# Order of the cross-attention weight products around an output projection, in a fused encoder layer

## The chip, the cores and the metric

The kernel runs on one core of a Trainium2 chip. The metric is the device time of one execution in microseconds; before the change it is 1414.73 us, the median of three runs (1414.48 to 1418.52).

The engines are called as in the profile: PE (TensorE, matrix products), DVE (VectorE), ACT (ScalarE), POOL (GpSimd) and SP (SyncE, which issues most loads). PE writes its results to PSUM, which has eight banks of 128 x 512 float32; DVE and ACT empty them.

## The reference

One encoder layer on 1024 tokens of width 1024, in float32, with 256 memory tokens:

```
x = x + rms_norm(concat(rms_norm(s5(u)), rms_norm(fox(q, k, v))) @ w_out)
h = rms_norm(x)
q = h @ wq                                   # 4 heads of 256
k, v = split(rms_norm(mem) @ wkv)            # 256 memory tokens
p = softmax(q k^T / 16) per head
x = x + rms_norm((p v, heads side by side) @ wo)
x = x + rms_norm(swiglu(rms_norm(x)))
```

s5 is a state-space mixer on half of the channels, fox a forgetting attention with 8 heads on the other half.

## The kernel before, in words

Products are made in about full precision: each operand is split into a high and a low part (`split`, L112: ACT copies the source into the rounded high part, DVE subtracts it from the source for the low part), and each product is three matmuls (`mm3`, L121: high x high, high x low, low x high; lines L122, L123, L124).

The cross-attention is rearranged so that no query or value matrix is made for the tokens. For each head, wq is multiplied by the keys beforehand (`build_a`, L993): one 1024 x 256 matrix per head that turns a token tile directly into scores. `build_a(0)` makes heads 0 and 1, `build_a(1)` heads 2 and 3; the result is kept in the tiles Ah and Al. In the same way each head's values are multiplied by its rows of wo (the "value weights", VW, L1207 to L1224), so that a token tile's softmax weights times VW gives the projected output directly.

The order around the change is this:

1. The forgetting attention runs with other work between its units (L1014 to L1016): the state-space branch's projections, the memory's keys and values (written to DRAM as kv_d), the SSM half of the output projection (written to DRAM as t1_d), and at its end `build_a(0)`.
2. The output projection's attention half (L1033 to L1058, "the projection loop"): eight tiles of 128 tokens in the order 3, 4, 5, 6, 7, 0, 1, 2, each in two half tiles of 512 columns. A half tile is twelve matmuls into one PSUM bank "x" (L1045). DVE adds the SSM half, fetched from t1_d into the tile t (L1039, called t_d in the profile), with the factor r_f per row (L1046); r_f exists only when the forgetting attention is complete. ACT sums squares (L1048), POOL multiplies by a gain row (L1050), and after both halves DVE makes the row's norm factor (L1052, L1053) and adds the residual (L1054). The tile goes to DRAM for tiles 3 to 7 (L1058) and is kept in SBUF for 0 to 2. After each half tile one step of `build_a(1)` is taken (L1051): a step is twelve matmuls of 256 columns. There are eight steps, so the written order has them in the first half of the loop.
3. The value weights of the four heads, one after the other (L1208 to L1224): 24 matmuls of 512 columns per head, in four banks (g for even heads, x for odd ones); the head's second half of the contraction (d = 1) follows after all four banks have had the first. Tile 0's norm is prepared and its transposes are made with the last head (L1210, L1222).
4. Scores, softmax and value products of the eight token tiles (from L1225), then the feed-forward layer.

Buffers: tiles with one tag share a few buffers, and a new tile waits until the oldest holder's last reader is done. Tag "a" has two, "b" two, "c" three, "e" one, "t2" three; weights are loaded into "raw" (two buffers; L158) and split into "whl" (three buffers; L163 to L164, whose splits are given priority). The t of the loop uses a, a, b, a, a, b, a, a (L1037). "slab" has sixteen buffers of 8 KB per partition; Ah, Al, the attention output yf, the matrix wo and VW live there. Some weights are staged in "e" instead of "raw" (argument `stage`).

The written order is not the queue's order. A planner arranges each engine's instructions when the kernel is complete: written order is the priority, and an instruction that the planner takes to be not ready yet lets a later one pass. After that each engine's queue is fixed, and what stands behind a waiting instruction on an engine waits with it. That holds for SP's list of loads too.

Of the kernel before, what the change touches and what calls it, by code (L numbers as in the profile page):

```python
# [10 lines left out]
F32R = mybir.dt.float32r  # L11
# [6 lines left out]
P = 128  # L18
S = 1024
D = 1024  # L20
KT = D // P
# [8 lines left out]
XH = 4  # L30
# [22 lines left out]
def layer(ctx: ExitStack, tc: tile.TileContext, a, out):  # L53
    nc = tc.nc
    dve, act, pool, pe, sp = nc.vector, nc.scalar, nc.gpsimd, nc.tensor, nc.sync
# [13 lines left out]
    def slab(shape, dt=F32R):  # L69
        return slabp.tile(shape, dt, name="slab", tag="slab")  # L70

    def whl(shape, dt=F32R):
        return whlp.tile(shape, dt, name="whl", tag="whl")

    def raw(shape):
        return rawp.tile(shape, F32, name="raw", tag="raw")

    def g_ps(shape):
        return psg.tile(shape, F32, name="g", tag="g")
# [4 lines left out]
    def sm(n, name):  # L84
        return small.tile([P, n], F32, name=name, tag=name)
# [26 lines left out]
    def split(hi, lo, src, mul=None, lo_eng=None):  # L112
        first = act.activation(out=hi, in_=src, func=AF.Copy, scale=1.0 if mul is None else mul)  # L113
        if mul is None:
            (lo_eng or dve).tensor_tensor(out=lo, in0=src, in1=hi.bitcast(F32), op=ALU.subtract)  # L115
        else:
            dve.scalar_tensor_tensor(out=lo, in0=src, scalar=mul, in1=hi.bitcast(F32),
                                     op0=ALU.mult, op1=ALU.subtract)
        return first

    def mm3(ps, lh, ll, rh, rl, first, last):  # L121
        pe.matmul(ps, lh, rh, start=first, stop=False)  # L122
        pe.matmul(ps, lh, rl, start=False, stop=False)  # L123
        pe.matmul(ps, ll, rh, start=False, stop=last)  # L124
# [29 lines left out]
    def load_w(src, shape, first=0, stage=None):  # L154
        w = tt(stage, [P, D]) if stage else raw([P, D])
        hl = whl([P, 2, D])
        if not first:
            sp.dma_start(out=w, in_=src)  # L158
        for cs in (slice(0, first), slice(first, D)):
            if cs.start < cs.stop:  # L160
                if first:
                    sp.dma_start(out=w[:, cs], in_=src[:, cs])
                with tc.high_priority(offset=boost):  # L163
                    split(hl[:, 0, cs], hl[:, 1, cs], w[:, cs])  # L164
        v = hl.rearrange("p t (a b) -> p t a b", b=shape)
        return v[:, 0], v[:, 1]
# [17 lines left out]
    kv_d = dram.tile([16, P, 256], F32, name="kv_d")  # L184
# [10 lines left out]
    def tt(tag, shape=None, dt=F32):  # L195
        return t4.tile(shape or [P, S], dt, name=tag, tag=tag, bufs=BUFS[tag])

    def t2t(shape, dt=F32):
        return tt("t2", shape, dt)
# [643 lines left out]
    def drain(*gens):  # L843
        gens = [g for g in gens if g is not None]
        while gens:
            for g in list(gens):
                try:
                    next(g)
                except StopIteration:
                    gens.remove(g)  # L850

    def step(g, n=1):
        for _ in range(n):
            if next(g, "end") == "end":
                return
# [89 lines left out]
    def gain_row(i, tag):  # L945
        g = tt(tag)
        sp.dma_start(out=g, in_=a["post_g"][i:i + 1, :].broadcast_to([P, D]))
        return g
# [26 lines left out]
    def fillers():  # L975
        yield from v1
        yield from glu(ys)
        mem = []
        rows = out_ssm(ys)
        step(rows)  # L980
        yield
        for _ in mem_load(r_mem[0], mem):
            step(rows)
            yield
        for i in range(16):
            mem_tile(i, *mem)
            yield
        yield from rows
        yield from build_a(0)
# [3 lines left out]
    def build_a(c):  # L993
        for t in range(2):
            Ah[c, t], Al[c, t] = slab([P, 4, 512]), slab([P, 4, 512])
        for h in range(2):
            hd = 2 * c + h
            kr = t2t([P, 2, 256])
            sp.dma_start(out=kr, in_=kv_d[2 * hd:2 * hd + 2].rearrange("d p m -> p d m"))
            kh = tt("ea"[h * (1 - c)], [P, 2, 2, 256], F32R)  # L1000
            split(kh[:, 0], kh[:, 1], kr)
            wq = [load_w(a["wqT"][2 * hd + d], P) for d in range(2)]
            ms = slice(h * 256, h * 256 + 256)
            for ft in range(0, KT, 2):
                ps = g_ps([P, 2, 256])
                for f in range(2):
                    for d in range(2):
                        mm3(ps[:, f], wq[d][0][:, ft + f], wq[d][1][:, ft + f], kh[:, 0, d], kh[:, 1, d], d == 0, d == 1)
                for f in range(2):
                    split(Ah[c, ft // 4][:, ft % 4 + f, ms], Al[c, ft // 4][:, ft % 4 + f, ms], ps[:, f],  # L1010
                          g_xa[:, ft + f:ft + f + 1])
                yield
# [7 lines left out]
    def x_ps(shape):  # L1020
        return psx.tile(shape, F32, name="x", tag="x")

    wo = []
# [4 lines left out]
        split(hl[:, 0], hl[:, 1], w)  # L1028
        wo.append(hl)
    g_mp = gain_row(0, "d")  # L1030
    a1 = build_a(1)
    kept = {}
    for n, j in enumerate((3, 4, 5, 6, 7, 0, 1, 2)):  # L1033
        ts = slice(j * P, (j + 1) * P)
        xt = tt("c")
        sp.dma_start(out=xt, in_=a["x"][ts, :])
        t = tt("aab"[n % 3])  # L1037
        for i in range(2):
            sp.dma_start(out=t[64 * i:64 * i + 64], in_=t1_d.rearrange("j (k s) d -> s k j d", s=16)[2 * j + i])  # L1039
        ss4, ss, r = sm(4, "ss4"), sm(1, "ss"), sm(1, "r")  # L1040
        for h in range(2):
            hs = slice(h * 512, h * 512 + 512)
            ps = x_ps([P, 512])
            for k in range(4):
                mm3(ps, yf[k][:, 0, ts], yf[k][:, 1, ts], wo[k][:, 0, hs], wo[k][:, 1, hs], k == 0, k == 3)  # L1045
            dve.scalar_tensor_tensor(out=t[:, hs], in0=ps, scalar=r_f[:, j:j + 1], in1=t[:, hs], op0=ALU.mult, op1=ALU.add)  # L1046
            for q in range(2 * h, 2 * h + 2):
                act.activation(out=tt("yt", [P, 256]), in_=t[:, q * 256:q * 256 + 256], func=AF.Square,  # L1048
                               accum_out=ss4[:, q:q + 1])
            pool.tensor_tensor(out=t[:, hs], in0=t[:, hs], in1=g_mp[:, hs], op=ALU.mult)  # L1050
            step(a1)  # L1051
        dve.tensor_reduce(out=ss, in_=ss4, op=ALU.add, axis=mybir.AxisListType.X)  # L1052
        rsqrt_mean(r, ss, D)  # L1053
        dve.scalar_tensor_tensor(out=xt, in0=t, scalar=r, in1=xt, op0=ALU.mult, op1=ALU.add)  # L1054
        if j < 3:
            kept[j] = xt
        else:
            stC.dma_start(out=x1_d[j], in_=xt)  # L1058


    drain(a1)
    def transpose_split(src, dst_h, dst_l):
        for k0 in range(0, KT, 4):
            tp = g_ps([P, 4, P])
            for k in range(4):
                pe.transpose(tp[:, k], src[:, (k0 + k) * P:(k0 + k + 1) * P], ident)  # L1066
            split(dst_h(k0), dst_l(k0), tp)
# [19 lines left out]
    def xa_turn(j):  # L1087
        transpose_split(xr[j][0], lambda k: xT[j][:, 0, k:k + 4], lambda k: xT[j][:, 1, k:k + 4])
# [27 lines left out]
    def xa_values(j, cc, between=None):  # L1116
        pT, t, ss2 = pts[j]
        ops = {c: g_ps([P, 512]) for c in cc}
        with ExitStack() as stack:
            for k in range(KT):  # L1120
                if k == 5 and between:
                    stack.enter_context(tc.issue_after(between().ins))
                for c in cc:
                    cs = slice(c * 512, c * 512 + 512)
                    mm3(ops[c], pT[:, 0, k], pT[:, 1, k], VW[k][:, 0, cs], VW[k][:, 1, cs], k == 0, k == KT - 1)
        for c in cc:
# [77 lines left out]
            dve.tensor_tensor(out=t[name], in0=x, in1=y, op=ALU.subtract)  # L1204
            done(name, t[name])

    VW = [slab([P, 2, D]) for _ in range(KT)]  # L1207
    for h in range(XH):  # L1208
        if h == 3:
            xa_prep(0)  # L1210
        vr = t2t([P, 2, 256])
        sp.dma_start(out=vr, in_=kv_d[8 + 2 * h:8 + 2 * h + 2].rearrange("d p m -> p d m"))
        vh = tt("b", [P, 2, 2, 256], F32R)
        split(vh[:, 0], vh[:, 1], vr)
        wo_ = [load_w(a["wo"][2 * h + d], 512, stage="e" if (2 * h + d) % 3 == 2 else None) for d in range(2)]
        tiles = [(mt, c, (x_ps if h % 2 else g_ps)([P, 512])) for mt in range(2) for c in range(2)]
        for d in range(2):
            for mt, c, ps in tiles:
                ms = slice(mt * P, mt * P + P)
                mm3(ps, vh[:, 0, d, ms], vh[:, 1, d, ms], wo_[d][0][:, c], wo_[d][1][:, c], d == 0, d == 1)  # L1220
        if h == 3:
            xa_turn(0)  # L1222
        for mt, c, ps in tiles:
            split(VW[2 * h + mt][:, 0, c * 512:c * 512 + 512], VW[2 * h + mt][:, 1, c * 512:c * 512 + 512], ps)  # L1224
    xa_prep(1)  # L1225
    for c in range(2):
        xa_scores(0, c)
# [388 lines left out]
```

## Time and profile before

| what | value |
|---|---|
| median of 3 runs | 1414.73 us |
| the profiled execution | 1412.18 us |
| its span, first to last instruction | 1410.4 us |
| mean granted clock of TensorE | 0.990 |
| DVE, ACT, POOL busy, share of the span | 68%, 46%, 27% |
| projection's matmuls, first and last start | 474.6 and 541.4 us |

The profile lists instructions with their start in microseconds from the span's start and with their line; `x<-whl,b` means that an instruction writes tile x and reads tiles whl and b. A helper's line, such as L122 or L115, is shared by all that call it, so the tile names tell which product or split it is: `g<-e,whl` at 256 columns is `build_a`, with the keys in "e"; `g<-whl,b` and `x<-whl,b` at 512 columns are value weights, with the values in "b"; `x<-slab` is the projection loop; `x<-slab,whl` after it are scores. In brackets stands the idle time of that engine before the instruction and what ended it. The duration of a matmul includes its way through the array; the distance from one start to the next is what a stream of them costs.

### The profile page before, as it was taken

How to read it: one execution, taken by the hardware profiler on the slowest of the kernel's cores; microseconds unless marked ns; L12 is line 12 of the kernel's file. 1: busy time of each engine (PE TensorE's matmuls, PEld its weight loads, DVE VectorE, ACT ScalarE, POOL GpSimd, SP SyncE). 2: the span in 40 equal slices, each digit the busy share in tenths (PEclk: the TensorE clock that was granted, in tenths of full speed). 3: DMA queues.
4: the chain of work that ended last, by engine and by line, in shares of the span. 5: the costliest groups of instructions: out<-in, count | busy, mean ns of one | idle time of the engine just before them, and what ended most of it. 6: DMA issues, size and time to landing. Idle time of an engine off the chain costs nothing.

```text
span 1410.4 us, 20272 instructions
## 1 busy us (share of the span) xinstructions
PE 1381.5 (98%) x7353; PEld 1163.3 (82%) x7353; DVE 952.1 (68%) x1719; ACT 652.8 (46%) x1289; POOL 378.7 (27%) x430
## 2 busy tenths in 40 slices
PE   9999999999999898999999999999999999999997
PEld 7889888889888786888888788888888888888886
DVE  8949945857666687545467767777776676555566
ACT  7383345666566555433344532333333334544351
POOL 0011110011111133001021377676766651000021
PEclk9999999889999999999999999999999999999999
DMA  6335665357562855024467345554444447965544
GB/s 217 91 107 162 204 224 135 91 165 224 187 180 95 214 185 201 1 83 159 147 213 250 102 174 195 186 173 168 144 159 151 162 150 244 344 203 194 179 165 164
DMA packets 104502, 239.45 MB, mean 170 GB/s; under 512 B 11465, under 2 KB 40137, under 8 KB 104273
## 3 DMA queue, kind: packets, MB, share of 16 engines
q1 hardware_dynamic: 85872, 176.24, 39.8%
q0 software_dynamic: 18528, 61.91, 12.3%
q8 instruction: 58, 0.95, 0.3%
q14 instruction: 44, 0.35, 0.1%
HBM read 169.43 MB, written 77.33 MB: 175 GB/s over the span
## 4 chain that ended last, share of the span: by engine, by line
PE 60%; DVE 1%; ACT 0%; issue 0%; DVEq 0%; ACTq 0%
PE x L1281 17%; PE g L1281 13%; PE x L1544 7%; PE g L1544 7%; PE x L123 2%; PE x L124 2%; PE g L122 2%; PE x L122 2%; PE g L124 2%; PE g L123 2%; PE g L1066 1%; PE g L1177 1%; DVE c L1054 0%; DVE whl L115 0%; ACT yt L1048 0%
## 5 line engine op out<-in xcount | busy, mean ns | idle before, releaser
L1281 PE MATMUL x<-slab,op 128*128 128x512 f32 x984 | 233.2, 389 | 0.5 <-DVE op L115 0.5
L1281 PEld LDWEIGHTS x<-slab,op 128*128 128x128 f32 x984 | 184.7, 188 | 39.2 <-DVE op L115 1.0
L1281 PE MATMUL g<-slab,op 128*128 128x512 f32 x744 | 178.7, 389 | 0.0
L115 DVE TENSOR_TENSOR slab<-slab 128x1024 fp32r<-128x1024 f32 (+2 forms) x92 | 110.6, 1208 | 86.6 <-ACT slab L113 84.4
L1281 PEld LDWEIGHTS g<-slab,op 128*128 128x128 f32 x744 | 139.7, 188 | 29.0
L122 PE MATMUL g<-slab,whl 128*128 128x512 f32 (+1 forms) x416 | 151.7, 365 | 0.8 <-ACT slab L485 0.4
L124 PE MATMUL g<-slab,whl 128*128 128x512 f32 (+1 forms) x416 | 148.9, 359 | 0.0
L123 PE MATMUL g<-slab,whl 128*128 128x512 f32 (+1 forms) x416 | 148.3, 356 | 0.0
L113 ACT ACTIVATE slab<-slab 128x1024 fp32r<-128x1024 f32 (+2 forms) x92 | 94.9, 1036 | 107.9 <-DMA slab<-hs_d 79.0
L1544 PE MATMUL g<-slab 128*128 128x512 f32 x462 | 126.6, 389 | 0.0
L1544 PE MATMUL x<-slab 128*128 128x512 f32 x462 | 126.6, 389 | 0.0
L1544 PEld LDWEIGHTS g<-slab 128*128 128x128 f32 x462 | 86.7, 188 | 18.0
L1544 PEld LDWEIGHTS x<-slab 128*128 128x128 f32 x462 | 86.7, 188 | 18.0
L115 DVE TENSOR_TENSOR op<-slab,op 128x512 fp32r<-128x512 f32 x80 | 84.4, 1066 | 11.6 <-ACT op L113 11.3
L1357 POOL TENSOR_TENSOR wt<-wt 128x256 f32<-128x256 f32 x88 | 83.0, 943 | 21.3 <-DMA wt<-in_w_down 18.0
L122 PEld LDWEIGHTS g<-slab,whl 128*128 128x128 f32 x416 | 78.6, 189 | 12.0 <-ACT whl L113 0.6
L124 PEld LDWEIGHTS g<-slab,whl 128*128 128x128 f32 x416 | 78.4, 189 | 11.7 <-DVE whl L115 0.2
L122 PE MATMUL g<-whl,slab 128*128 128x256 f32 (+2 forms) x288 | 86.8, 310 | 1.2 <-ACT yt L318 0.7
L123 PEld LDWEIGHTS g<-slab,whl 128*128 128x128 f32 x416 | 78.6, 189 | 10.8
L113 ACT ACTIVATE op<-slab 128x512 fp32r<-128x512 f32 x80 | 50.0, 627 | 79.3 <-PE x L1281 38.0
L124 PE MATMUL g<-whl,slab 128*128 128x256 f32 (+2 forms) x288 | 85.9, 299 | 0.0
L123 PE MATMUL g<-whl,slab 128*128 128x256 f32 (+2 forms) x288 | 85.9, 298 | 0.0
(385 smaller groups left out, 2890.6 us busy)
## 6 DMA issues: line engine op xcount, KB each, us to landing
hs_d<-ev POOLq DMA_DIRECT2D x77, 256.0 KB, 2.6
slab<-hs_d SPq DMA_DIRECT2D x35, 512.0 KB
wt<-in_w_down SPq DMA_DIRECT2D x44, 256.0 KB
wt_d<-wt POOLq DMA_DIRECT2D x22, 512.0 KB, 5.1
slab<-in_w_gate SPq DMA_DIRECT2D x20, 512.0 KB
slab<-in_w_up SPq DMA_DIRECT2D x20, 512.0 KB
slab<-wt_d SPq DMA_DIRECT2D x20, 512.0 KB
wd_d<-in_w_down SPq DMA_DIRECT2D x33, 256.0 KB
```

Source lines behind the costliest of these rows:

```text
L113: first = act.activation(out=hi, in_=src, func=AF.Copy, scale=1.0 if mul is None else mul)
L115: (lo_eng or dve).tensor_tensor(out=lo, in0=src, in1=hi.bitcast(F32), op=ALU.subtract)
L122: pe.matmul(ps, lh, rh, start=first, stop=False)
L123: pe.matmul(ps, lh, rl, start=False, stop=False)
L124: pe.matmul(ps, ll, rh, start=False, stop=last)
L1066: pe.transpose(tp[:, k], src[:, (k0 + k) * P:(k0 + k + 1) * P], ident)
L1177: turned = pe.transpose(tp[:, k], h3[:, (4 * n + k) * P:(4 * n + k + 1) * P], ident)
L1281: pe.matmul(ps, x[:, k], y[:, k], start=first and k + n == 0, stop=k == 3 and n == 2, skip_group_check=not first)
L1357: pool.tensor_tensor(out=o, in0=x, in1=y, op=ALU.subtract)
L1544: pe.matmul(banks[n][j], xo[:, u, js], wo[:, v], start=ends[0] and k == 0, stop=ends[1] and k == 2, skip_group_check=onto is not None)
```

## The change

The value weights of heads 0 and 1 take the place of `build_a(1)` between the half tiles, and `build_a(1)` is made after the loop, in one piece, ahead of the value weights of heads 2 and 3. The value weights become a generator with a step of three matmuls: eight steps per head, sixteen for two heads, one after each of the sixteen half tiles. Within a head the column half is now the outer loop, with two banks at a time, and the two banks are split as soon as their half is complete. Heads 0, 1 and 2 use g banks and head 3 uses x banks. The split operands move to other tags: the values of heads 0 to 3 to b, e, e, b, the keys of heads 2 and 3 to b and a. No weight is staged in "e" by the value weights any more. The transposes of token tile 0 (`xa_turn(0)`) come after the last value split, where they came before it.

```
-            kh = tt("ea"[h * (1 - c)], [P, 2, 2, 256], F32R)
+            kh = tt(("ea", "ba")[c][h], [P, 2, 2, 256], F32R)
...
-    a1 = build_a(1)
+    VW = {}
+
+    def value_weights(h):
+        vr = t2t([P, 2, 256])
+        sp.dma_start(out=vr, in_=kv_d[8 + 2 * h:8 + 2 * h + 2].rearrange("d p m -> p d m"))
+        vh = tt("beeb"[h], [P, 2, 2, 256], F32R)
+        split(vh[:, 0], vh[:, 1], vr)
+        wo_ = [load_w(a["wo"][2 * h + d], 512) for d in range(2)]
+        for mt in range(2):
+            VW[2 * h + mt] = slab([P, 2, D])
+        for c in range(2):
+            tiles = [(mt, (x_ps if h == 3 else g_ps)([P, 512])) for mt in range(2)]
+            for d in range(2):
+                for mt, ps in tiles:
+                    ms = slice(mt * P, mt * P + P)
+                    mm3(ps, vh[:, 0, d, ms], vh[:, 1, d, ms], wo_[d][0][:, c], wo_[d][1][:, c], d == 0, d == 1)
+                    yield
+            for mt, ps in tiles:
+                split(VW[2 * h + mt][:, 0, c * 512:c * 512 + 512], VW[2 * h + mt][:, 1, c * 512:c * 512 + 512], ps)
+
+    def first_values():
+        for h in range(2):
+            yield from value_weights(h)
+
+    between = first_values()
...
-            step(a1)
+            step(between)
...
-    drain(a1)
+    drain(between)
...
-    VW = [slab([P, 2, D]) for _ in range(KT)]
-    for h in range(XH):
+    drain(build_a(1))
+    for h in range(2, XH):
         if h == 3:
             xa_prep(0)
-        vr = t2t([P, 2, 256])
-        sp.dma_start(out=vr, in_=kv_d[8 + 2 * h:8 + 2 * h + 2].rearrange("d p m -> p d m"))
-        vh = tt("b", [P, 2, 2, 256], F32R)
-        split(vh[:, 0], vh[:, 1], vr)
-        wo_ = [load_w(a["wo"][2 * h + d], 512, stage="e" if (2 * h + d) % 3 == 2 else None) for d in range(2)]
-        tiles = [(mt, c, (x_ps if h % 2 else g_ps)([P, 512])) for mt in range(2) for c in range(2)]
-        for d in range(2):
-            for mt, c, ps in tiles:
-                ms = slice(mt * P, mt * P + P)
-                mm3(ps, vh[:, 0, d, ms], vh[:, 1, d, ms], wo_[d][0][:, c], wo_[d][1][:, c], d == 0, d == 1)
-        if h == 3:
-            xa_turn(0)
-        for mt, c, ps in tiles:
-            split(VW[2 * h + mt][:, 0, c * 512:c * 512 + 512], VW[2 * h + mt][:, 1, c * 512:c * 512 + 512], ps)
+        drain(value_weights(h))
+    xa_turn(0)
     xa_prep(1)
```

## The prediction

> **What bounds the kernel now.** The page comes first: TensorE (PE) is busy for nearly the whole span, so the time can fall only where PE stands still or runs slowly, and must rise wherever new idle time appears.
>
> ```profile
> span 1410.4 us, 20272 instructions
> PE 1381.5 (98%) x7353; PEld 1163.3 (82%) x7353; DVE 952.1 (68%) x1719; ACT 652.8 (46%) x1289; POOL 378.7 (27%) x430
> ```
>
> Second, the chain of PE's own instructions in order of time gives the stages. The first product of the value weights starts where the output projection's last matmul ends, and the first score product starts where the value weights and the transposes end.
>
> ```profile
> 514.97 0.28 PE L122 MATMUL g<-e,whl 128*128 128x256 f32 x1
> 515.93 0.28 PE L124 MATMUL g<-e,whl 128*128 128x256 f32 x1
> 541.66 0.39 PE L122 MATMUL g<-whl,b 128*128 128x512 f32 x1
> 547.10 0.39 PE L122 MATMUL x<-whl,b 128*128 128x512 f32 x1
> 553.88 2.08 PE L122 MATMUL x<-whl,b 128*128 128x512 f32 x4 [1.74 <-ACT whl L113]
> 567.97 1.03 PE L1066 MATMUL g<-ident,c 128*128 128x128 f32 x8
> 572.51 0.50 PE L122 MATMUL x<-slab,whl 128*128 128x512 f32 x1
> ```
>
> Third, the busy times by stage: the projection loop after its row factors are known, the stage behind it, that stage's second part, and five microseconds inside it (columns: PE, weight loads, DVE, ACT, POOL, granted clock, DMA share, GB/s).
>
> ```profile
> 499.84:541.66 41.82, 40.90 (x208) 34.66 (x207) 32.90 (x62) 23.00 (x82) 21.28 (x17) 1.00 0.68 225
> 541.66:572.51 30.85, 27.25 (x113) 20.85 (x111) 26.11 (x46) 22.67 (x54) 5.84 (x4) 0.89 0.31 108
> 553.77:572.51 18.74, 18.34 (x76) 14.44 (x76) 18.50 (x32) 16.94 (x34) 0.00 (x0) 0.84 0.26 84
> 555.00:560.00 5.00, 4.71 (x13) 3.25 (x12) 5.00 (x8) 4.82 (x9) 0.00 (x0) 0.54 0.54 178
> ```
>
> The loop is full: 40.90 of 41.82 us. The stage behind it is not. It holds 96 value matmuls; 24 of them take 547.10 - 541.66 = 5.44 us, so 0.227 us each and 21.8 us in all. Sixteen transposes add about 2 us (eight in 1.03). That is 23.8 us of PE work in 30.85 us: 7 us are lost, partly in waits, partly because the clock fell to 0.54. The reader should also see the DVE column: 18.50 of 18.74 us in the second part. There DVE is the limit, not PE.
>
> Fourth, the waits there (first PE's in total, then single instructions of PE, DVE, SP's queue and ACT with the idle time before them) say what begins the trouble.
>
> ```profile
> PE x L122 <- ACT whl L113: 1.7, 1, 1.7
> PE x L122 <- DVE a L1046: 1.6, 2, 1.1
> 536.07 0.50 PE L122 MATMUL x<-slab 128*128 128x512 f32 x1 [0.92 <-DVE rsv L139]
> 548.27 0.75 DVE L1046 SCALAR_TENSOR_TENSOR a<-x,r_f,a 128x512 f32<-128x512 f32 x1 [2.33 <-DMA a<-t_d]
> 539.88 0.58 SPq L1039 DMA_DIRECT2D a<-t_d  x1
> 532.97 1.06 ACT L113 ACTIVATE whl<-e 128x1024 fp32r<-128x1024 f32 x1 [3.56 <-DMA e<-in_wo]
> 552.78 1.04 ACT L113 ACTIVATE whl<-raw 128x1024 fp32r<-128x1024 f32 x1
> ```
>
> The last projection tile's SSM half was requested at 539.88 and used at 548.27. Until then DVE (L1046) and ACT (squares, L1048) stood still, PE ran into x banks that L1046 had not emptied, and the split of a value weight waited until 552.78. Earlier, ACT had stood 3.56 us before the load staged in "e", which delayed the tile whose "a" buffer the last one takes over.
>
> **The change, part by part.** On PE nothing is added or removed. The second half of wq times keys (build_a(1)) is 96 matmuls of 256 columns, eight steps of which take 515.93 - 514.97 = 0.96 us, so 0.12 each, 11.5 us in all. The value weights of heads 0 and 1 are 48 of 512 columns, 48 x 0.227 = 10.9 us. They change places, so the loop holds 0.6 us less and the stage behind it 0.6 us more. The PE work behind the loop until the first score product becomes 11.5 + 10.9 + 1.0 (the eight transposes of tile 0) = 23.4 us.
>
> In the loop. The steps are three matmuls after each of 16 half tiles instead of twelve after each of the first eight. The wait before 536.07 (0.9) should go, since a half tile now has 0.7 us of other work behind it throughout: gain 0.9, bounds 0 to 0.9. Against it, before 499.84 (no row factor, four x banks full) the old filler had 48 narrow matmuls (5.8 us); four new steps have 2.7 us. If the planner does not pull steps five to eight forward, PE waits: 0 to 3.0 us. I take 0, as it moved narrow steps out of their written place already.
>
> ```profile
> 463.19 1.19 SPq L1039 DMA_DIRECT2D b<-t_d  x2
> 535.27 0.74 DVE L1046 SCALAR_TENSOR_TENSOR b<-x,r_f,b 128x512 f32<-128x512 f32 x1
> SPq L947 <- POOL a L1050: 6.5, 1, 6.5
> ```
>
> Buffers and queues. Head 0's values now occupy one "b", so the projection tile whose half was fetched at 463.19 must wait for their release, halfway through the loop (an estimate: near 520). It is used at 535.27, some 15 us later, and the last tile's half took 8.4 us (539.88 to 548.27): cost 0, or up to 2 if transfers pile up there. No weight is staged in "e" any more: ACT's 3.56 us stop goes, which should bring the last tile's request forward by about 3 us. The gain row of L1069 stays ahead of the moved wq loads in SP's written order and waits 6.5 us for POOL; loads planned behind it start late. Cost 0 to 6.5, taken as 0 because the two wo loads behind it now cost PE nothing either. The second key operand takes an "a" buffer, so it waits for the projection's seventh tile; cover is the first head's 5.8 us of matmuls. The slabs needed in the loop stay four. xa_turn(0) moves behind the last split: 0 to 1.5 us (two 0.6 us splits and a start), covered if the planner pulls the transposes forward as it does now.
>
> The decisive term is DVE behind the loop. These rows price its parts.
>
> ```profile
> 522.83 1.31 DVE L117 SCALAR_TENSOR_TENSOR slab<-g,gains,slab 128x256 fp32r<-128x256 f32 x3
> 561.37 2.48 DVE L115 TENSOR_TENSOR slab<-x,slab 128x512 fp32r<-128x512 f32 x4
> L115 DVE TENSOR_TENSOR whl<-raw,whl 128x1024 fp32r<-128x1024 f32 x4 | 4.9, 1219 | 0.0
> L1054 DVE SCALAR_TENSOR_TENSOR c<-b,r,c 128x1024 f32<-128x1024 f32 x1 | 1.3, 1286 | 0.1
> L113 ACT ACTIVATE whl<-raw 128x1024 fp32r<-128x1024 f32 x4 | 4.2, 1060 | 0.2 <-DVE slab L115 0.2
> ```
>
> From 541.66 to 572.51 DVE did 26.1 us. The moved product brings 16 low parts of 0.44 us: +7.0. One more weight is split behind the loop (six, not five): +1.2. Of 14 value-weight low parts before the first score product, about nine remain (two of head 1, four of head 2, three of head 3): -5 x 0.62 = -3.1. With an earlier last tile, one L1046 (0.75) and one L1054 (1.29) fall into the loop: -2.0. Sum 29.2 us. That is more than PE's 23.4, so **the bound behind the loop is DVE**, which has work from the loop's end on. With the loop ending 0.9 + 0.6 us earlier, at 540.1 or so, the first score product starts at 540.1 + 29.2 = 569.3 instead of 572.5: **3.2 us gained**. DVE's idle time there, 30.85 - 26.1 = 4.7 us now, is taken as 0, as DVE's list is longer now than PE's; if it all came back the sum would be a loss of 1.5. If the value splits are put off instead, it is the first rival. Behind that point the instructions are the same.
>
> The profiled execution took 1412.18 us, 1.8 above its span and 2.6 below the median of the three runs, 1414.73. The same difference on that median gives 1414.7 - 3.2 = 1411.5.
>
> The clock: 0.54 in the quoted five microseconds, after waits of at most 1.7 us. With PE 23.4 us busy of 29.2 it should hold, so I add no clock loss; DVE hides any. The Trainium skill ("TensorE: Matmul & The Clock Gate", section "Why this matters for your kernels") asks only for no idle gaps over about 3 us between bursts. The trace disagrees: its longest gap there is 1.74 us. [...]
>
> **The rivals.**
>
> *PE becomes the bound (faster).* Value splits of heads 2 and 3 are first needed by the value product, several score products later. If seven more are put off (7 x 0.62 = 4.3), DVE needs 24.9 us and the scores start at 565.0: 7.5 gained, 1407.2. For it: the planner already left some splits behind 572.51. Against it: all eight PSUM banks hold value tiles then, and the scores need one of theirs.
>
> *The ring of three weight buffers (slower).* A weight's split takes 1.06 on ACT and 1.22 on DVE, 2.28 us after its buffer is free. In the stage behind the loop, four weights (the second of each key head's successor, and both of head 3) get buffers only when the product before them ends. The new order, column half outermost, leaves six matmuls (1.4 us) as cover where the old left twelve. PE has 572.5 - 540.1 - 23.4 = 9.0 us to lose before the change is slower, 2.3 per weight. If each also queues behind four value low parts (2.5 us), it costs 2.28 + 2.5 - 1.4 = 3.4, four 13.6: the scores start at 577.1, 4.6 late, or 1419.3. For it: ACT's split that stood until 552.78. Against it: the planner interleaves partial products of several banks. The same page's section "Architectural detail" says that ACT and DVE are strict FIFO and only weight loads are pulled ahead on PE; that would make this rival the rule, and the quoted split behind a late transfer agrees.
>
> *The order written is not the order run.* The planner decides by readiness; if it bunches the value steps and delays the rest as now, the loss merely moves: 1414.7.
>
> **How the numbers follow.** Forecast 0.42, PE-bound 0.28, ring 0.20, unchanged 0.10. A measurement here can tell about 0.3%, 4.2 us. Faster: 0.26 of the PE-bound case, 0.09 of the forecast, 0.01: 0.36. Slower: 0.18 of the ring, 0.02 of the others: 0.20. The rest, 0.44, is within. The forecast alone spans 1408 to 1416 (splits put off in part; idle time back). The range takes in most of the PE-bound case and the ring up to its computed price: 1406.5 to 1420.
>
> **What would show it.** Right: 16 groups of three 512-column value matmuls in the loop; the narrow products between about 541 and 553; DVE busy for over 95% from there to the first score product, near 570; the clock at 1.0 throughout. The first step fails if PE waits near 500, the second if the last tile's SSM half still lands at 548. PE over 95% busy there and scores before 567 mean the first rival; waits of PE on splits of whl of over 2.3 us each mean the second. The whole is wrong if a difference of more than 2 us appears outside 470 to 575 us.

## The result, and the profile after

The changed kernel takes 1412.69 us (median of 15 runs, 1410.39 to 1413.98), the kernel before beside it 1414.93 us (15 runs, 1411.87 to 1420.03). The ratio is 0.9983, 95% interval 0.9975 to 0.9992: 0.17% faster, 2.2 us by the medians, inside the 0.3% that was called "same", and in the direction of the forecast (3.2 us).

The two profiled executions do not show this gain by their totals: 1412.18 us before, which was 2.6 under the median of its first three runs, and 1412.68 after. The comparison has to be made stage by stage, and with care: a second execution of each kernel, further down, shows that the stretch compared here varies by about 2 us in either kernel, as much as the effect. The page of the kernel after begins:

```profile
span 1410.8 us, 20277 instructions
PE 1379.8 (98%) x7353; PEld 1162.4 (82%) x7353; DVE 950.5 (67%) x1719; ACT 652.5 (46%) x1289; POOL 384.9 (27%) x430
```

Two stages matter: from the first projection matmul to the end of the projection loop, and from there to the first score product. The busy times by stage of the kernel before have this row for the first one (the prediction shows the second, 541.66 to 572.51):

```profile
474.59:541.66 67.07, 63.57 (x355) 53.34 (x354) 45.85 (x84) 35.11 (x103) 23.51 (x19) 1.00 0.67 223
```

and the kernel after has these (columns as before: length, then PE, weight loads, DVE, ACT, POOL, granted clock, DMA share, GB/s):

```profile
477.01:500.00 22.99, 22.99 (x136) 18.79 (x135) 14.04 (x23) 11.44 (x26) 2.48 (x3) 1.00 0.64 216
477.01:538.93 61.92, 61.92 (x307) 50.96 (x306) 43.07 (x70) 29.78 (x90) 25.34 (x20) 1.00 0.68 212
538.93:572.92 33.99, 27.09 (x161) 23.73 (x160) 28.78 (x54) 24.62 (x59) 4.38 (x3) 0.95 0.40 124
538.93:557.00 18.07, 11.21 (x73) 10.14 (x72) 16.73 (x30) 11.52 (x32) 4.38 (x3) 0.91 0.57 176
557.00:572.92 15.92, 15.88 (x90) 13.59 (x90) 12.05 (x24) 13.10 (x27) 0.00 (x0) 1.00 0.21 66
553.00:557.00 4.00, 2.97 (x14) 2.97 (x15) 3.38 (x5) 1.03 (x3) 0.00 (x0) 0.57 0.50 131
```

The loop is 5.15 us shorter (67.07 to 61.92) and has no idle time of PE at all. The stage behind it is 3.14 us longer (30.85 to 33.99). PE's idle time has moved: 3.50 us in the loop before (67.07 - 63.57) and 3.60 behind it (30.85 - 27.25); after, 0.00 and 6.90. Of the 2.0 us by which this pair differs (97.92 to 95.91), 1.7 can be put down to the clock: behind the loop it was granted at 0.89 over 30.85 us, a loss of 3.4, and now at 0.95 over 33.99, a loss of 1.7.

Where the loop's idle time went is read from single instructions. In the kernel before, PE waited twice in the loop besides the wait at 536.07 that the prediction names; first its own rows, then ACT's and SP's behind the first of them:

```profile
477.08 0.73 PE L122 MATMUL x<-slab 128*128 128x512 f32 x2 [1.55 <-ACT slab L113]
490.59 0.38 PE L122 MATMUL g<-e,whl 128*128 128x256 f32 x1 [1.03 <-ACT whl L113]
475.97 1.06 ACT L113 ACTIVATE slab<-raw 128x1024 fp32r<-128x1024 f32 x1 [5.05 <-DMA raw<-in_w_out_f]
453.50 0.35 SPq L1026 DMA_DIRECT2D raw<-in_w_out_f  x1
455.63 1.31 SPq L1039 DMA_DIRECT2D b<-t_d  x2
459.22 1.22 SPq L1039 DMA_DIRECT2D a<-t_d  x2
464.48 0.39 SPq L1026 DMA_DIRECT2D raw<-in_w_out_f  x1
```

The wait at 477.08 is the fourth projection matmul, the first that needs the second block of w_out_f. That block was requested at 464.48, behind three tiles of t of 512 KB each: the two above and the one at 463.19 that the prediction shows. ACT stood 5.05 us for it. In the kernel after, the same stretch of SP and ACT:

```profile
453.91 0.34 SPq L1026 DMA_DIRECT2D raw<-in_w_out_f  x1
460.74 1.30 SPq L1063 DMA_DIRECT2D a<-t_d  x2
465.61 1.19 SPq L1063 DMA_DIRECT2D b<-t_d  x2
466.90 0.39 SPq L1026 DMA_DIRECT2D raw<-in_w_out_f  x1
474.15 1.06 ACT L113 ACTIVATE slab<-raw 128x1024 fp32r<-128x1024 f32 x1 [0.80 <-DMA raw<-in_w_out_f]
```

Only two tiles of t stand ahead; the third is requested at 501.03, because head 0's value operand has its "b" buffer. From request to split the second block takes 7.25 us (466.90 to 474.15) where it took 11.49 (464.48 to 475.97), and PE does not wait.

Behind the loop PE of the kernel after waits five times, each time for DVE:

```profile
538.93 0.28 PE L122 MATMUL g<-b,whl 128*128 128x256 f32 x1
540.93 0.39 PE L124 MATMUL g<-b,whl 128*128 128x256 f32 x1 [1.25 <-DVE whl L115]
544.70 0.39 PE L122 MATMUL g<-b,whl 128*128 128x256 f32 x1 [1.24 <-DVE slab L115]
548.18 0.39 PE L122 MATMUL g<-b,whl 128*128 128x256 f32 x1 [1.78 <-DVE slab L115]
551.25 0.39 PE L122 MATMUL g<-a,whl 128*128 128x256 f32 x1 [1.36 <-DVE slab L117]
554.03 0.58 PE L124 MATMUL g<-a,whl 128*128 128x256 f32 x1 [1.23 <-DVE whl L115]
572.92 0.49 PE L122 MATMUL x<-slab,whl 128*128 128x512 f32 x1
```

These are 6.86 us, all in the first half of the stage, where the narrow key products stand beside the last two projection tiles, the last value splits of the loop and the weights' splits. DVE is busy 16.73 of 18.07 us there. From 557 on it is the other way round: PE 15.88 of 15.92, DVE 12.05.

### The profile page after: what moved, and what is told of

Same layout as the page of the kernel before. It is cut to its first block, busy times and chain, and to the rows that moved or that the text cites. A ratio compares the mean times of both kernels' runs of the same rounds, so it can differ in the third digit from the quotient of the medians.

```text
span 1410.8 us, 20277 instructions
## 1 busy us (share of the span) xinstructions
PE 1379.8 (98%) x7353; PEld 1162.4 (82%) x7353; DVE 950.5 (67%) x1719; ACT 652.5 (46%) x1289; POOL 384.9 (27%) x430
## 4 chain that ended last, share of the span: by engine, by line
PE 60%; DVE 0%; ACT 0%; issue 0%; DVEq 0%
PE x L1293 17%; PE g L1293 13%; PE x L1556 7%; PE g L1556 7%; PE g L124 2%; PE g L122 2%; PE g L123 2%; PE x L124 2%; PE x L122 2%; PE x L123 2%; PE g L1090 1%; PE g L1201 1%; DVE whl L115 0%; DVE c L1078 0%; DVE x L1536 0%
## 5 line engine op out<-in xcount | busy, mean ns | idle before, releaser
L1369 POOL TENSOR_TENSOR wt<-wt 128x256 f32<-128x256 f32 x88 | 85.9, 976 | 18.6 <-DMA wt<-in_w_down 15.2
L115 DVE TENSOR_TENSOR op<-slab,op 128x512 fp32r<-128x512 f32 x80 | 81.3, 1026 | 11.6 <-ACT op L113 11.3
```

What stands on the lines that cost most here:

```text
L1369: pool.tensor_tensor(out=o, in0=x, in1=y, op=ALU.subtract)
```

## The experiments

Two theories were tried first: A, that the gain is made in the loop by what stands between the half tiles, and B, that it depends on when PE reaches the loop. From the third set on a third stood beside them, C: the gain comes from the place of one load. The ratios come from 10 to 15 runs of the kernel, those of after_back and spread_late from 5. This table has, for each profiled execution, PE's wait at the fourth projection matmul, the length of the loop (first projection matmul to the end of the last), the stretch from there to the first score product, and their sum (us); the ratio is to the kernel before, timed beside it.

| kernel | ratio [95%] | wait at the fourth | loop | behind | sum |
|---|---|---|---|---|---|
| before | 1 | 1.55 | 67.2 | 30.7 | 97.9 |
| before_again | 1.0002 [0.9989, 1.0015] | 2.73 | 67.5 | 32.1 | 99.6 |
| after | 0.9983 [0.9975, 0.9992] | none | 61.4 | 34.5 | 95.9 |
| after_again | 0.9989 [0.9974, 1.0005] | none | 63.3 | 34.6 | 98.0 |
| spread | 0.9975 [0.9963, 0.9988] | 4.38 | 71.9 | 26.8 | 98.7 |
| no_e | 0.9991 [0.9978, 1.0004] | 3.92 | 70.0 | 31.1 | 101.1 |
| after_pool | 1.0001 [0.9990, 1.0011] | none | 63.1 | 36.0 | 99.1 |
| bunched | 1.0003 [0.9992, 1.0014] | none | 62.6 | 36.7 | 99.3 |
| late_t | 0.9980 [0.9970, 0.9991] | none | 64.8 | 32.2 | 97.0 |
| after_back | 1.0034 [1.0020, 1.0047] | 4.29 | 71.4 | 32.5 | 103.9 |
| spread_late | 0.9948 [0.9936, 0.9960] | none | 65.1 | 25.7 | 90.9 |
| spread_b | 0.9985 [0.9972, 0.9998] | none | 62.5 | 33.3 | 95.7 |
| after_swap | 1.0016 [1.0005, 1.0027] | none | 63.7 | 37.0 | 100.7 |
| after_mixed | 0.9984 [0.9972, 0.9997] | none | 63.5 | 33.5 | 96.9 |

(In after the loop's last three value matmuls come behind the last projection matmul, 0.5 us; that is why 61.4 stands here and 61.92 above.)

**before_again and after_again**: both kernels of the case once more, unaltered.

> The kernel before, once more, to see how far its stages move from execution to execution. Marks: the first projection matmul to the last one's successor (loop), and from there to the first score product (behind); 67.1 and 30.9 us in its first profile. Theory A (the change's gain is made in the loop: no waits of PE there): the ratio is 1.000 and the loop again takes 66 to 68 us, however early PE arrives. Theory B (the loop was only shorter after the change because PE came 2.4 us later to it in that execution, so that its loads were there): a profile in which PE arrives later shows a loop of 65 us or less in the kernel before too.

> The changed kernel once more: loop 61.9 and behind it 34.0 us in its first profile, ratio 0.9983. Theory A: loop within 1 us of 61.9 whenever PE arrives, ratio 0.997 to 0.999. Theory B: if PE arrives at 474.6 as in the first profile of before, the loop takes 64 us or more and the whole stage gains nothing.

The second executions tell what belongs to a kernel and what to an execution. Both times before waits at the fourth matmul and after does not; both times the stage behind the loop is over 2 us longer in after. The sum does not repeat so well: 97.9 and 99.6 us before, 95.9 and 98.0 after. In before_again the wait is longer, and the clock falls behind it; first PE's row, then the busy times of 4 us there:

```profile
482.66 1.22 PE L122 MATMUL x<-slab 128*128 128x512 f32 x2 [2.73 <-ACT slab L113]
```

```profile
482.00:486.00 4.00, 3.34 (x9) 2.59 (x10) 3.36 (x6) 2.17 (x5) 0.00 (x0) 0.57 0.61 222
```

That speaks against theory B for this wait: PE reached the loop at 479.0 in this execution, later than in any other, and still waited, while after_again reached it at 474.1 and did not.

**spread**: the kernel before, with the key products of heads 2 and 3 in sixteen half steps, one after each half tile, as the change has them for the value weights.

```
                 for f in range(2):
                     for d in range(2):
                         mm3(...)
+                    if c == 1 and f == 0:
+                        yield
```

> The kernel before with build_a(1) taken in sixteen steps of six narrow matmuls, one after each half tile, instead of eight of twelve; nothing else is changed, and the value weights stay behind the loop. Theory A with evenness as its cause: the loop loses its wait near the end (0.9 us) and the last tile's half comes no later, so the loop is 1 to 3 us shorter; the stage behind keeps its 31 us or gets shorter; ratio 0.996 to 0.999. Rival (it matters which product stands there, since the narrow one's splits load DVE and its weights come late): no gain, ratio 0.999 to 1.002.

The ratio, 0.9975, is at least as good as the change's, without one wide product in the loop. The profiled execution shows the stage behind the loop at 26.8 us and full clock, against 30.7 and 32.1 before; in the loop it has the longest wait of all at the fourth matmul and another of 2.26 us. It is also the slowest of its twelve (1415.25 us, median 1411.51), so its sum, 98.7, does not show the gain that the ratio shows.

**no_e**: the kernel before with no weight staged in "e".

```
-        wo_ = [load_w(a["wo"][2 * h + d], 512, stage="e" if (2 * h + d) % 3 == 2 else None) for d in range(2)]
+        wo_ = [load_w(a["wo"][2 * h + d], 512) for d in range(2)]
```

> The kernel before with no value weight staged in the tag e (all in raw); nothing else is changed. If ACT's 3.56 us stop before the staged load is what delays the last tile's SSM half, that half is used 2 to 4 us earlier than at 548.3 and the stage behind the loop shrinks by 2 to 3 us: ratio 0.998. If the transfers themselves are late, whatever their place: ratio 1.000 within 0.001, and the last half is used at 547 or later.

The two waits behind the loop stay, 1.17 and 1.73 us where the kernel before has 1.12 and 1.74:

```profile
551.12 0.51 PE L122 MATMUL x<-whl,b 128*128 128x512 f32 x1 [1.17 <-DVE a L1046]
553.83 2.08 PE L122 MATMUL x<-whl,b 128*128 128x512 f32 x4 [1.73 <-ACT whl L113]
```

The ratio's interval includes 1. ACT's stop of 3.56 us before the staged load is gone, but the last tile's half is still used at 548.18 us (548.27 before): the staging is not what bound that stage.

**after_pool**: the kernel after, with the low parts of the second weight of each head split by POOL behind the loop, to relieve DVE.

```
-            wq = [load_w(a["wqT"][2 * hd + d], P) for d in range(2)]
+            wq = [load_w(a["wqT"][2 * hd + d], P, lo_eng=pool if c and d else None) for d in range(2)]
```

(and the same for `wo` of heads 2 and 3)

> The changed kernel with the low part of the second weight (d = 1) of each head behind the loop made on POOL instead of DVE: four parts of 1.22 us leave DVE. If DVE is the bound behind the loop, as forecast, that stage shrinks from 34.0 us by 2 to 5 us, ratio to before 0.995 to 0.997. If DVE only takes turns with PE (it stands when PE catches up), the gain is under 1.5 us; if POOL's longer part (a 512-column product takes it 1.3 us) comes on the path, the stage grows by up to 2 us.

POOL needs 2.36 to 2.78 us for what DVE does in 1.22, and PE waits 1.50 us for one of these splits. PE's longest wait there becomes 3.91 us, for DVE, and the gain is gone. DVE's work behind the loop fell only from 28.78 to 27.88 us, not by the 4.9 of the four parts; why is not shown. So the attempt does not tell whether less DVE work would help.

**bunched**: the kernel after with two steps of the value weights after each of the first eight half tiles (`step(between, 2)`).

> The changed kernel with two value steps after each of the first eight half tiles and none after the last eight; nothing else is changed. If the even spread is what keeps PE from waiting in the loop, waits on x banks return near the end of the loop (about 1 us) and ratio is 0.999 to 1.001. If the spread does not matter (only which product stands there, and what stands behind), the loop stays free of waits and the ratio stays at 0.997 to 0.999; the weights for the stage behind come free earlier, so that stage may even lose a microsecond.

```profile
555.85 0.58 PE L122 MATMUL g<-a,whl 128*128 128x256 f32 x1 [9.12 <-DVE slab L117]
```

The loop keeps its gain (62.6 us), as the second branch of the expectation had it, but the ratio is 1.0003, as the first had it: nearly all of PE's idle time behind the loop is one wait of 9.12 us. DVE had stood 2.92 us for the seventh tile's t, until 543.10, and worked off the last two tiles ahead of the splits that PE needed. What this variant gains in the loop it loses behind it.

**late_t**: the kernel before with one thing altered, the place of the third t load on SP.

```
-        sp.dma_start(out=w, in_=a["w_out_f"][i])
+        last_w = sp.dma_start(out=w, in_=a["w_out_f"][i])
...
-            sp.dma_start(out=t[64 * i:64 * i + 64], in_=t1_d...)
+            with tc.issue_after(last_w.ins) if n == 5 else ExitStack(): sp.dma_start(out=t[64 * i:64 * i + 64], in_=t1_d...)
```

> The kernel before, with nothing altered but the place of one load on SP: the two DMAs of the sixth projection tile's t (the second tile in b, used late in the loop) are issued behind the last w_out_f load instead of between the second and the third; the order of PE, DVE, ACT and POOL is that of before. Theory C (the change's gain comes from this load: in the traces of before it stands ahead of the w_out_f loads, ACT waits for them, and PE waits 1.55 us at the fourth projection matmul, 2.73 in the second execution, 3.92 and 4.38 in two variants, with a stretch at half clock behind it in three of four): the wait there falls under 1 us, there is no half clock between the loop's start and 490 us, the stretch from the first projection matmul to the loop's end is 2 to 5 us shorter than in before, and the ratio is 0.996 to 0.999. Theory A (the gain comes from the wide value products taking the place of the narrow key products in the loop): the wait at the fourth matmul stays as it is, ratio 0.9995 to 1.0015. Theory D (the wait comes of the time at which PE reaches the loop): the wait is there or not, whatever the load's place, ratio 0.999 to 1.001.

On PE, DVE, ACT and POOL the order of instructions is that of the kernel before. (`issue_after` puts SP's load behind the one named.) SP's list now has the sixth tile's t behind w_out_f, and ACT stands 1.69 us for the second block instead of 5.05:

```profile
466.98 0.35 SPq L1026 DMA_DIRECT2D raw<-in_w_out_f  x1
474.87 3.08 SPq L1026 DMA_DIRECT2D raw<-in_w_out_f  x2
478.00 1.23 SPq L1039 DMA_DIRECT2D b<-t_d  x2
475.27 1.06 ACT L113 ACTIVATE slab<-raw 128x1024 fp32r<-128x1024 f32 x1 [1.69 <-DMA raw<-in_w_out_f]
```

PE does not wait there any more. The loop and the stage behind it, which keeps its waits and its lower clock:

```profile
477.24:542.05 64.81, 63.71 (x356) 53.73 (x355) 44.90 (x83) 33.23 (x98) 23.40 (x19) 1.00 0.70 224
542.05:574.20 32.15, 27.11 (x114) 20.34 (x112) 26.16 (x46) 22.46 (x55) 5.83 (x4) 0.89 0.32 103
```

The ratio is 0.9980 (0.9970 to 0.9991). Within the intervals this one load gives as much as the whole change.

**after_back**: the kernel after with head 0's values in "e" (`"eeeb"` for `"beeb"`), so that t gets its "b" back.

> The kernel after, with head 0's value operand in buffer e instead of b, so that both value operands of the loop stand one after the other in the one e buffer and the two b tiles of the loop are free for t again, as in before. Theory C (the load's place): the sixth tile's t is loaded ahead of the last w_out_f loads again, PE waits 1.5 to 4.5 us at the fourth projection matmul, half clock may follow it, and head 1's operand waits besides some 1 to 3 us in the middle of the loop for the one e buffer; ratio 1.000 to 1.003 to the kernel before, 1.002 to 1.005 to the kernel after. Theory A (the wide products): the wait at the fourth matmul stays away; only the wait in the middle of the loop, 1 to 3 us, is added, ratio 0.998 to 1.0005 to the kernel before.

The wait is back, with the load that causes it:

```profile
462.70 1.19 SPq L1063 DMA_DIRECT2D b<-t_d  x2
478.22 1.06 ACT L113 ACTIVATE slab<-raw 128x1024 fp32r<-128x1024 f32 x1 [7.79 <-DMA raw<-in_w_out_f]
479.33 1.10 PE L122 MATMUL x<-slab 128*128 128x512 f32 x2 [4.29 <-ACT slab L113]
```

The second value head now also needs the one "e" that the first holds, and PE waits 2.10 us in the middle of the loop (that the one comes of the other is not shown), so the 1.0034 is not the load's price alone. With late_t, where nothing else was touched, the cause of the loop's main wait is settled from both sides.

**spread_late**: spread and late_t together.

> The kernel spread (before, with the key products of heads 2 and 3 cut into sixteen half steps, ratio 0.9975) and the same later place of the sixth tile's t load as in late_t. Theory C: the two gains lie at different places (wait and half clock at 478 to 487 us here, the stretch behind the loop there) and add up: no wait above 1 us at the fourth projection matmul, no half clock between 476 and 490 us, from the first projection matmul to the first score product 92 to 95 us where spread has 98.8; ratio 0.992 to 0.996, under both kernels of the case. Theory A or D: no change beside spread, ratio 0.996 to 0.999.

```profile
476.23:541.38 65.15, 63.26 (x351) 52.88 (x350) 47.05 (x87) 33.09 (x104) 24.63 (x21) 1.00 0.69 223
541.38:567.11 25.73, 25.03 (x119) 19.81 (x117) 24.40 (x44) 22.46 (x48) 2.76 (x2) 1.00 0.39 124
```

The two gains add up: 1406.68 us against 1414.36, ratio 0.9948 (0.9936 to 0.9960), faster than both kernels of the case. PE idles 2.59 us in the whole stretch (90.88 - 88.29), where before had 7.1, and the clock stays at 1.00. The stretch, 90.9 us, is shorter than the 92 to 95 expected.

**spread_b**: spread with its second key operand in "b", so that t's load must move by itself.

```
-            kh = tt("ea"[h * (1 - c)], [P, 2, 2, 256], F32R)
+            kh = tt(("ea", "eb")[c][h], [P, 2, 2, 256], F32R)
```

> The kernel spread, with the key operand of the second of its two heads in buffer b instead of the one buffer e. Two things should come of it: the wait of 2.26 us of PE in the middle of spread's loop, where that head's operand waits for e, goes; and, as the operand takes a b, the sixth projection tile's t must wait for its buffer and its load moves behind the w_out_f loads without being told to. Theory C: both gains, from the first projection matmul to the first score product 90 to 95 us; ratio 0.991 to 0.996. Theory A or D: only the first gain, ratio 0.995 to 0.998. If the late t load itself holds PE up (the tile's product waits for it, or the last value head's operand waits for b), a new wait of over 1 us shows at that tile and the ratio stays at 0.997 or above.

This was expected to come near spread_late and did not: 0.9985. The loop has no wait. But the sixth tile's t, tied to its buffer, is now requested at 517.58 us (476.32 in spread_late), and DVE waits at the loop's end for the seventh tile's:

```profile
540.02 0.75 DVE L1048 SCALAR_TENSOR_TENSOR a<-x,r_f,a 128x512 f32<-128x512 f32 x1 [5.98 <-DMA a<-t_d]
```

What DVE could not do then, it does behind the loop: 30.88 us of work there, against 24.40 in spread_late, and PE is idle for 5.1 of 33.3 us. This is near the third clause of the expectation, one tile later. Moving a load by taking its buffer moves it as far as the buffer says, not as far as one wants. That this made the seventh tile late is not shown: its t was requested at 527.82 us, only 1.4 us later than in spread_late, yet first used 6.2 us later (540.02 against 533.84).

**after_swap and after_mixed**: the kernel after with the third value head ahead of the key products behind the loop, or in turn with them.

```
-    drain(build_a(1))
-    for h in range(2, XH):
-        if h == 3:
-            xa_prep(0)
-        drain(value_weights(h))
+    drain(value_weights(2))
+    drain(build_a(1))
+    xa_prep(0)
+    drain(value_weights(3))
```

(after_mixed steps `build_a(1)` and `value_weights(2)` alternately, with the latter in x banks.)

> The kernel after, with the third value head's wide products put ahead of the key products behind the loop (third value head, both key heads, first x half, fourth value head) instead of behind them. In after PE waits 6.9 us in all between 540 and 554 us, for DVE and for splits on DVE and ACT, while the narrow key products run there beside the last projection tile's tail, and the stretch from the loop's end to the first score product is 34.5 us against 30.7 to 32.3 in before. Theory G (the order does it: narrow products, which ask for a split after every 1.4 us of PE work, stand where DVE has most to do besides): the sum of the waits there falls under 4 us, the stretch is 30 to 32.5 us, ratio 0.995 to 0.9975. Theory H (the amount of DVE work behind the loop does it, in whatever order): the waits move to another place, the stretch stays at 33.5 to 35.5 us, ratio 0.9975 to 0.9995.

> The kernel after, with the third value head's wide products and the key products behind the loop taken step by step in turn, as far as the three weight buffers allow (in PE's order the first key head still stands first, and the wide products lie between those of the second key head). Theory G (the order does it): the waits from the loop's end to the first score product fall from 6.9 us to 3 to 5 us, because only the first key head still stands at the loop's tail, stretch 31 to 33.5 us, ratio 0.996 to 0.998. Theory H (the amount of DVE work does it): stretch 33.5 to 35.5 us, ratio 0.9975 to 0.9995. If the two heads' four weights wait for the three weight buffers, a new wait for a split into whl of over 1.5 us appears and the ratio is over 0.999.

```profile
548.59 0.80 PE L122 MATMUL g<-whl,e 128*128 128x512 f32 x1 [8.00 <-ACT e L113]
```

after_swap ran into a wait that no theory had: the third head's operand needs the one "e", which head 1 holds until the loop ends, and PE stands 8.00 us for it. It tells nothing of G against H. after_mixed does, by its busy times:

```profile
540.43:573.89 33.46, 27.44 (x163) 22.69 (x163) 29.87 (x54) 25.87 (x61) 4.70 (x4) 1.00 0.40 130
```

PE is idle for 6.0 us, nearly as long as in after, and DVE's work is of the same size (29.87 us); the ratio is 0.9984. That lies on theory H's edge: the order alone did not bring the stretch under 33 us. What remains open is how short the stage behind the loop can be with wide products in the loop and fewer DVE instructions behind it; no run had that.

## Why the prediction was right, and where its steps failed

The forecast (1411.5 us, same) lay 1.2 us from the median, but that closeness is luck: two of its steps were wrong in opposite directions. It had the loop 1.5 us shorter and the stage behind it 1.7; the traces have 5.15 shorter and 3.14 longer.

*The loop, forecast 1.5 us shorter.* Mis-sized: 5.15 us. The wait at 536.07 went, as forecast. The sum lacked the other two waits: 1.55 us at 477.08 and 1.03 at 490.59, which went too. PE's work in the loop fell 1.65 us where 0.6 was counted; the rest was not resolved. The step taken at 0, PE waiting before 499.84, was right: PE is busy 22.99 of 22.99 us to 500, because the planner did pull the later value steps forward: eighteen value matmuls stand in a row from 497.44. The sign "16 groups of three" therefore did not hold: three groups come before these eighteen, and seven behind them, from 517.84 on.

*The moved "b" load, "cost 0, or up to 2 if transfers pile up there".* This step failed, and in its sign. It looked only at where the load went, not at what it had stood in front of. There, as late_t shows, it delayed w_out_f, ACT and the fourth projection matmul; late_t prices its removal at a ratio of 0.9980 by itself. The price could have been worked out from the trace of before, where the stretch ahead of the loop reads

```profile
453.00:475.00 22.00, 20.39 (x163) 16.80 (x162) 17.37 (x38) 13.63 (x30) 1.83 (x2) 1.00 0.86 192
```

At 192 GB/s a tile of 512 KB takes 2.7 us (an estimate from this row), and ACT stood 5.05 us for the block behind it.

*No weight staged in "e".* The last tile's half was used at 541.54, not 548.27, so the tile came even earlier than forecast; but no_e, with the tile used at 548.18, shows that the staging was not what held it. What brought its request forward in after was not isolated.

*The decisive term, DVE behind the loop.* The amount was right, 28.78 us of DVE work measured and 29.2 forecast, though partly by terms that cancel: seven weights' low parts ran there, not six, and seven value low parts, not nine. PE's 23.4 left out eight transposes, about 1 us: all sixteen still ran in this stage. The conclusion failed at "DVE's idle time there ... is taken as 0": it is 5.21 us (33.99 - 28.78), so the stage takes 34.0 and not 29.2, and DVE is busy for 85% of it, not over 95%. The prediction priced this case itself, as the return of 4.7 us. The rows of the two halves point to the cause: DVE has 16.73 us of work in the first 18.07, PE 15.88 in the last 15.92. The bound changes hands in the middle, and a sum over the whole stage for one engine misses what the other adds after that.

*The clock, forecast at 1.0 throughout.* Wrong: 0.57 from 553 to 557, at the end of five waits of which the longest is 1.78 us. That is 1.7 us lost. As in the kernel before, the rule of the Trainium skill ("TensorE: Matmul & The Clock Gate", section "Why this matters for your kernels") that there be no idle gaps over about 3 us between bursts does not cover what this trace shows.

*The rivals.* The ring of weight buffers was there in small: two waits of PE on splits of whl, 1.25 and 1.23 us, not four of 3.4. The PE-bound case holds from 557 us on only. "The loss merely moves", the rival given 0.10, describes the pair of traces well as to PE's idle time (7.1 us before, 6.9 after), though not for the reason given there. Beyond the first score product nothing differs: from there to the end it is 837.9 us in both. Ahead of the loop the pair does differ by more than the 2 us that were named as a sign against the whole, 474.59 to 477.01; but after_again reaches the loop at 474.08 and before_again at 478.99, so this does not belong to the change.

*The wide products themselves* add nothing that these runs can tell: late_t has the load's new place without them and stands at 0.9980, the change at 0.9983. Together with spread this points to the change's gain being the load's, and to what the sixteen steps gain behind the loop in spread being spent in after on the key products that stand there. after_back, the change without the load's move, agrees: less its new wait of 2.10 us and about 1.7 for the half clock behind it (0.59 from 524 to 528 us) it would take 1417.64 - 3.8 = 1413.8 us beside 1414.36 for the kernel before, hardly a gain (an estimate from these rows). No run has the one without the other.

## What to carry to other kernels

When a change gives a buffer to another tile, look at every load that waits for that buffer, and at both ends of its move: the transfers it will meet, and the transfers it no longer stands in front of. Sum a stage in parts where the bound may change hands, since two engines that are each the limit for half of it take longer than either list alone. When small gains at different places are found, try them alone and together: here two edits of one line or two each give 0.2 to 0.25%, and both give 0.52%.

## What the runs showed of the hardware that was not expected

The clock falls to half (0.50 from 553.50 to 555.50 us in the kernel before) after waits under 3 us: after one of 2.73 us at the fourth matmul (before_again, 0.57 over 4 us), and at the end of five of at most 1.78 us (after). A single one of 1.55 us (before, 477.08) left it at 1.00, and so did after_mixed's 6.0 us of idle time behind the loop, whose longest wait is 1.40 us. The time at half clock seems to come in pieces of one length: 0.57 over 4.00 us is 2 x 0.43 x 4.00 = 3.4 us at half, and 0.89 over the 30.85 us behind the loop in before is 6.8, twice as much. The Trainium skill ("TensorE: Matmul & The Clock Gate", section "What's actually happening") states a free-running window of 3413 ns; the trace agrees with that length.

Executions of one kernel differ by more than the effect: the first projection matmul starts at 474.6 us in one execution of the kernel before and at 479.0 in the other, though it is the same program. Single stages vary too: from there to the first score product it is 97.9 and 99.6 us before, 95.9 and 98.0 after. Traces tell where PE waits and for what; whether a kernel is faster is told by the ratio of many runs.
